# Scores inside chunks in two visits of four and three levels, and the pairs' seven products reordered with one bank for each two-part sum

## The chip, the cores and the metric

The kernel runs on one core of a Trainium2 chip. The metric is device time in microseconds (us) of one execution; lower is better. The core has a matrix engine (TensorE, in the profile PE for matmuls and PEld for weight loads), three other compute engines (VectorE = DVE, ScalarE = ACT, GpSimd = POOL), a queue for transfers (SyncE = SP), an on-chip memory, and PSUM, eight banks of 128 x 512 fp32 into which TensorE writes its products and from which DVE and ACT read them.

## The reference

One block on 1040 tokens (16 meta tokens and 1024 others) of width 1024: a norm, one wide projection, a pooling mixer beside chunked gated linear attention, gates, an output projection, and a squared-ReLU MLP. The change touches the projection and the attention's work inside a chunk of 64 tokens (4 heads, 64 key and 128 value channels each):

```python
z = jnp.einsum('bld,dn->bln', u, w_in)
a, q, k, v, r, lr, ga, gb = jnp.split(z, IN_SPLITS, axis=-1)
...
b = jnp.cumsum(ac, axis=2)
decay = jnp.exp(-jnp.abs(b[:, :, :, None, :] - b[:, :, None, :, :]))
scores = jnp.einsum('bhtk,bhsk,bhtsk->bhts', qc, kc, decay)
o = jnp.einsum('bhts,bhsv->bhtv', scores, vc) + jnp.einsum('bhtk,bhkv->bhtv', qc * jnp.exp(b), S)
```

Each score has a decay of its own for every pair of tokens and key channel, so `scores` isn't a plain product.

## The kernel before

Stages follow each other: norm, transposes and value projection (`start`), the first projections (`first_products`), **the projections in pairs with the scores between them (`pairs_of_projections`, some 141 to 376 us)**, the states across chunks, the output projection and the MLP. The change is in the third one.

*Products.* An fp32 matrix is split into a high and a low part (`split`, L977: ACT copies to the high part, L982, DVE subtracts it for the low part, L983), and `mm3` (L296) makes a product from three matmuls for each of 4 slices of the contraction, 12 of 128 x 512 (L300 to L302). The order on TensorE is the program's own (`manual_schedule` for PE); the order on DVE, ACT, POOL and SP in this stage is set by the framework's planner, and each of these engines works its own queue in order.

*Pairs.* Eleven pairs of 128-column weight blocks (`PAIRS`, L959: q, four of the gate gb, four of ga, two of r) are each multiplied by seven products P1 to P7 in place of eight (a Strassen-Winograd scheme). P1 and P2 add up in one bank (`xb`), P5 and P3 in another (`zb`), while P6, P7 and P4 take banks of tag `y` in turn. From these DVE makes `u2` (P1 + P6), `u3` (u2 + P7), and the four results: P1 + P2 (read from `xb` at P2's end), `zb` + u3 (L1102, after P5 and P7), P4 + u3 (L1112) and `zb` + u2 (L1116, after P3). They go through `put_q`, `put_gate` or `put_r` (ACT's tanh at L942, for r also a DVE product) to memory. `pairs_order` (L1006) sets the order P6 P1 P7 P5 P4 P2 P3, in which P1, P5 and P2 belong to the pair after that of the others. Two banks lie under the tag `sc`, two under `z`, two under `y`, two under `gs`.

*Weights of the products.* `sums_weights` (L1014) makes sums of weight blocks on GpSimd in halves (L1018) and splits them, three products ahead (`ahead`), into four slots. P5's sum is made into `fs`, P6's follows in place from it, P7's difference goes to `s3`, P3's again into `fs`. The next pair but one is loaded after P3.

*Scores.* `inside(p, half)` (L1208) is a unit: two heads, 512 tokens; there are four. It loads k, q (into two thirds of the tile `gi`) and the decay g, and builds operands for six levels of a binary tree over the 64 tokens: `grow` (L1229) makes level l + 1's operand pair from level l's with two DVE products (L1235, L1237), an ACT copy (L1236) and a small product of the decays (L1239), first from L1224 and L1227, at the end `last` (L1241). A level's score product (`scores`, L1191) is 16 matmuls on 64 x 64 quarters of the array, which the profile lists as 32; the first one has no decay (the token itself). They go to half of the two banks `gs`, half by half in turn. The first result is copied into `gi` by ACT (L1258), the others are laid in under a mask by DVE (`inlay`, L1255). Operands alternate between two tiles N, so a level's `grow` overwrites what the score product of the level before read. The filled `gi` goes to memory (L1279), and the next unit's loads go into the same tile (L1217 to L1219).

*How both are woven.* After each product with n > 8, `credit` grows by 12 x 512 / 2400 / 1.9 = 1.347, and while it is positive the chain `insides` goes on by a step, whose `yield` is taken off. A **visit** is a step in which TensorE makes score products. A unit has four of them: own and level 0, levels 1 and 2, levels 3 and 4, level 5. After each of the first two units `meta_state` makes that head pair's state from the meta tokens, with a transpose (L1177) and two small products (L1184), each in a step of its own.

Of the kernel before, what the change touches and what calls it, by code (L numbers as in the profile page):

```python
# [14 lines left out]
P = 128  # L15
D = 1024
SEQ = 1024
META = 16
# [10 lines left out]
VP = 272  # L29
NPAIR = DFF // P // 2  # L30
MP = 264
PACE, LEVEL, OPENING, STRETCH = 1.3, 1.6, 6.0, 1.9


class Stack:
# [87 lines left out]
def kernel(  # L123
# [30 lines left out]
    def bank(tag):  # L154
        if tag == "sc":
            sc_n[0] += 1
            return two("sc")[:, sc_n[0] % 2]
        return psp[tag].tile([P, 512], F32, name=f"b_{tag}", tag=tag)

    def two(tag):  # L160

        if tag in ("sc", "gs"):
            if tag not in wide:
                wide[tag] = psp[tag].tile([P, 2, 512], F32, name=f"b_{tag}", tag=tag)
            return wide[tag]
        return psp[tag].tile([P, 2, 512], F32, name=f"b_{tag}", tag=tag)
# [837 lines left out]
                    yield p, n  # L1004

    def pairs_order(n_pairs):  # L1006
        yield from (("P1", 0), ("P4", 0), ("P2", 0), ("P5", 0))
        for i in range(1, n_pairs + 1):
            for p in ("P6", "P1", "P7", "P5", "P4", "P2", "P3"):
                n = i if p in ("P1", "P5", "P2") else i - 1  # L1010
                if n < n_pairs and (p, n) != ("P4", 0):
                    yield p, n

    def sums_weights(order, n_pairs, load, eng):  # L1014

        def tt(out, a, b, op):
            for k in (slice(0, 2), slice(2, 4)) if eng is pool else (slice(0, 4),):
                eng.tensor_tensor(out[:, k], a[:, k], b[:, k], op)  # L1018

        for p, i in order(n_pairs):  # L1020
            a11, a12 = (w1raw[i, 0][:, k : k + 4] for k in (0, 4))
            if p in ("P1", "P2"):
                s = a11 if p == "P1" else a12
            else:
                a21, a22 = (w1raw[i, 1][:, k : k + 4] for k in (0, 4))
                s = None if p == "P4" else quad(S["fs"][:, i % 2] if p != "P7" else S["s3"])
                if p == "P5":
                    tt(s, a21, a22, ALU.add)
                elif p == "P6":
                    tt(s, s, a11, ALU.subtract)  # L1030
                elif p == "P7":
                    tt(s, a11, a21, ALU.subtract)
                elif p == "P3":
                    tt(s, a12, s, ALU.subtract)
                elif p == "P4":
                    s = a22
            yield p, i, split(s)
            if p == "P3" and i + 2 < n_pairs:
                load(i + 2, 0)
                load(i + 2, 1)  # L1040
# [8 lines left out]
    def first_pair():  # L1049
        raw.lend(*S["rawp"])  # L1050
        raw.slots = raw.slots[2:] + raw.slots[:2]
        raw.n = 0
        load_pair(0, 0)
        load_pair(0, 1)
        w1_slots()
        S["pw"] = sums_weights(pairs_order, len(PAIRS), load_pair, pool)

    def pair_weights():
        yield from S["first"]
# [2 lines left out]
    def pairs_of_projections():  # L1062
# [3 lines left out]
        S["fs"] = right.push("fs", [P, 2, HALF], F32)  # L1066
        S["s3"] = right.push("s3", [P, HALF], F32)
        S["u2p"] = right.push("u2p", [P, 2, HALF], F32)
        S["u3p"] = right.push("u3p", [P, 2, HALF], F32)
        load(1, 0)  # L1070
        load(1, 1)
        S["N"] = [right.push(f"n{i}", [P, HALF, 2], F32) for i in range(2)]
        S["F"] = right.push("f", [P, HALF, 2], F32)
        S["ends"] = right.push("ends", [P, HALF], F32)
        S["g"] = right.push("g", [P, HALF], F32)
        S["gi"] = right.push("gi", [P, 3, HALF], F32)
        banks(keep=1, y=2, gs=1, z=2)
        x, xb, zb = S["xs"], {}, {}
        total = 7 * len(PAIRS)
        chain, credit = insides(), 0.0  # L1080
        for n, (p, i, (ah, al)) in enumerate(ahead(pair_weights(), 3)):
            bh, bl = x[p]
            if p in ("P1", "P2"):
                b = xb[i] = bank("sc") if p == "P1" else xb[i]
            elif p in ("P5", "P3"):
                b = zb[i] = bank("z") if p == "P5" else zb[i]
            else:
                b = bank("y")
            more = p in ("P2", "P3")
            mm3(b, 4, lambda k: (ah[:, k], al[:, k]), lambda k: (bh[:, k], bl[:, k]), first=not more, more=more)  # L1090
            u2, u3 = S["u2p"][:, i % 2], S["u3p"][:, i % 2]
            put, d = PAIRS[i][1:]
            if p == "P1":
                act.activation(u2, b, ACT.Copy)
            elif p == "P2":
                put(d, 0, xb.pop(i), None)
            elif p == "P6":
                dve.tensor_tensor(u2, b, u2, ALU.add)
            elif p == "P7":
                dve.tensor_tensor(u3, b, u2, ALU.add)  # L1100
                c = nxt("c")
                dve.tensor_tensor(c, zb[i], u3, ALU.add)  # L1102
                put(d + 1, 1, c, c)
                if i == 0:
                    c = nxt("c")
                    dve.tensor_tensor(c, S["ends"], u3, ALU.add)
                    put(d + 1, 0, c, c)
            elif p == "P4" and i == 0:
                act.activation(S["ends"], b, ACT.Copy)
            elif p == "P4":  # L1110
                c = nxt("c")
                dve.tensor_tensor(c, b, u3, ALU.add)  # L1112
                put(d + 1, 0, c, c)
            elif p == "P3":
                c = nxt("c")
                dve.tensor_tensor(c, zb.pop(i), u2, ALU.add)  # L1116
                put(d, 1, c, c)
            if n > 8:
                credit += 12 * 512 / 2400 / STRETCH
# [44 lines left out]
        dve.tensor_tensor(sv[:, :, 0], sv[:, :, 0], end(1), ALU.add)  # L1164
        dve.tensor_tensor(pv[:, :, 1], pv[:, :, 1], end(0), ALU.add)

    def meta_state(p):
        pre, suf, y, km = (metab[:, i] for i in (META_LOG[p], 1, 2, 4))
        nc.sync.dma_start(km, k_dram[p, :, :META])
        dve.memset(suf, 0.0)  # L1170
        for m in (1, 2, 4, 8):
            twice(pre, suf, m)
        act.activation(y, suf, ACT.Exp, scale=1.0 / TAU)
        dve.tensor_tensor(y, y, km, ALU.mult)
        yield 5.0
        b = two("gs")[:, 0]
        pe.transpose(b[:META, :P], y, ident)  # L1177
        kt = gB[32 : 32 + META, 2 * 256 : 2 * 256 + P]
        dve.tensor_copy(kt, b[:META, :P])
        yield 2.0  # L1180
        b = two("gs")[:, 0]
        for e in range(2):
            r = slice(e * CH, (e + 1) * CH)
            pe.matmul(  # L1184
                b[r, :P], kt[:, r], vm[:, (2 * p + e) * P : (2 * p + e + 1) * P], start=True, stop=True,
                tile_position=(32, e * CH),
            )
        dve.tensor_copy(S["S"][:, 0, p], b[:, :P])
        yield 1.0

    def scores(kk, qq):  # L1191


        turn_n[0] += 1
        c = (turn_n[0] % 2) * 4 * CH
        b = two("gs")[:, :, c : c + 4 * CH].rearrange("p e (j t) -> p e j t", j=4)
        for j in range(4):
            for e, u in QUARTERS:
                r, to, s = part(e), part(u), part(2 * j + u)
                pe.matmul(b[to, e, j], kk[r, s], qq[r, s], start=True, stop=True, tile_position=(e * CH, u * CH))  # L1200
        return b
# [6 lines left out]
    def inside(p, half):  # L1208
# [8 lines left out]
        nc.sync.dma_start(gi[:, 1], k_dram[p, :, at : at + HALF])  # L1217
        nc.sync.dma_start(gi[:, 2], q_dram[p, half])
        nc.sync.dma_start(g, decay_dram[p, half])  # L1219
        yield 4.5  # L1220
        pairs = lambda a: a.rearrange("p (b u) n -> p b u n", u=2)
        plain, gp = kq.rearrange("p n (b u) -> p b u n", u=2), g.rearrange("p (b u) -> p b u", u=2)
        for u, to, other in ((1, N[0], F), (0, F, N[0])):
# [25 lines left out]
                act.activation(o[:, :, 1 - u], f[:, :, 1 - u], ACT.Copy)  # L1249
            dve.tensor_tensor(e2, ev[:, :, 0], ev[:, :, 1], ALU.mult)  # L1250

        yield 2.0

        def inlay(lvl, b):
            dve.copy_predicated(scc, mask[:, lvl : lvl + 1, None, :].broadcast_to([P, 2, 4, CH]), b)  # L1255

        b = [scores(kq[:, 0], kq[:, 1]), scores(N[0][:, :, 0], N[0][:, :, 1])]
        act.activation(scc, b[0], ACT.Copy)  # L1258
        inlay(0, b[1])
        e, at = g, 0  # L1260
        for lvl in range(6):
            m, n = 1 << lvl, N[lvl % 2]
            to = at + HALF // (2 * m)
            e2 = ends[:, at:to] if lvl < 5 else dec_of(p, half)
            if lvl < 5:
                grow(m, n, N[1 - lvl % 2], e, e2)
            e2_of, e, at = (e, e2), e2, to
            if lvl < 5:
                yield LEVEL
            if lvl in (1, 3):  # L1270
                b = [scores(N[i][:, :, 0], N[i][:, :, 1]) for i in (1, 0)]
                for i in range(2):
                    inlay(lvl + i, b[i])
            elif lvl == 5:
                b = scores(n[:, :, 0], n[:, :, 1])
                last(n, *e2_of)
                inlay(5, b)
        yield LEVEL
        nc.sync.dma_start(gi_dram[p, half], gi)  # L1279

    def insides():
        for half in range(2):
            for p in range(2):
                yield from inside(p, half)
                if half == 0:
                    yield from meta_state(p)

    step(one, pairs_of_projections)

# [660 lines left out]
```

## Time and profile before

| | |
|---|---|
| median of 3 runs (lowest, highest) | 1198.33 us (1198.26, 1198.54) |
| profiled execution, its own time | 1198.67 us |
| its span | 1195.8 us |
| granted TensorE clock, mean | 0.998 |
| HBM read and written | 128.66 and 62.93 MB, 160 GB/s over the span |

The profile shows one execution. For an engine it gives the time that it was busy, the share of the span and the instructions; for a group of instructions the line, engine, operation, out<-in by the program's names, shapes, count, busy time, mean ns of one, and the idle time just before them with what ended it. In a timeline each row has start and duration; matmuls are pipelined, so a duration reaches past the next one's start and the pace is read from starts. Of TensorE's chain that ended last 69% of the span is TensorE's own work.

### The profile page before, as it was taken

Reading aid. Unit: us, or ns where it says so; the run is one execution under the profiler, and the core shown is the slowest. Engines: PE = TensorE matmul, PEld = TensorE weight load, DVE = VectorE, ACT = ScalarE, POOL = GpSimd, SP = SyncE. Lnnn points to the kernel's source line nnn. Section 1 sums busy time; section 2 is a strip of 40 time slices with the busy share of each in tenths; the row PEclk is TensorE's granted clock in tenths of the full one; section 3 lists DMA queues with packets and bytes.
Section 4 is the critical chain, followed back from the end, with each engine's and each line's share of the span. In section 5 each row is a group of like instructions: output and inputs, shape, how many; then the busy total and the mean of one; then the engine's idle time right before and its main releaser. Section 6 shows DMA issues by size and latency. Waiting matters only on the chain.

```text
span 1195.8 us, 18439 instructions
## 1 busy us (share of the span) xinstructions
PE 1182.6 (99%) x6823; PEld 982.5 (82%) x6823; DVE 853.6 (71%) x1400; ACT 579.0 (48%) x1006; POOL 102.1 (9%) x121
## 2 busy tenths in 40 slices
PE   9999999999999999999999999999999999999997
PEld 7999887777778887888788888888888888888886
DVE  7679657565676779527986766777675887887686
ACT  7566544444456224216754555545454444445454
POOL 0224232333220000000000000000000000000000
PEclk9999999999999999999999999999999999999999
DMA  8232533434357879712254544445389963333532
GB/s 247 69 89 81 180 112 113 143 125 142 124 168 265 293 229 306 257 34 89 89 185 143 165 146 163 153 139 167 132 285 336 328 213 97 97 97 97 168 97 88
DMA packets 151001, 192.79 MB, mean 161 GB/s; under 512 B 12088, under 2 KB 85616, under 8 KB 150912
## 3 DMA queue, kind: packets, MB, share of 16 engines
q1 hardware_dynamic: 150752, 191.56, 50.1%
q8 instruction: 53, 0.87, 0.3%
q14 instruction: 36, 0.29, 0.1%
q10 hardware_dynamic: 160, 0.07, 0.0%
HBM read 128.66 MB, written 62.93 MB: 160 GB/s over the span
## 4 chain that ended last, share of the span: by engine, by line
PE 69%; DVE 3%; issue 1%; ACT 1%; DMA 0%; DVEq 0%
PE b_oa L300 5%; PE b_oa L302 5%; PE b_oa L301 5%; PE b_y L300 4%; PE b_mm L300 4%; PE b_y L301 4%; PE b_y L302 4%; PE b_mm L302 4%; PE b_mm L301 4%; PE b_ob L300 4%; PE b_ob L302 4%; PE b_ob L301 4%; PE b_z L301 3%; PE b_z L300 3%; PE b_z L302 3%; PE b_sc L300 2%
## 5 line engine op out<-in xcount | busy, mean ns | idle before, releaser
L300 PE MATMUL b_z<-th,w1h 128*128 128x512 f32 x240 | 94.3, 393 | 0.0
L301 PE MATMUL b_z<-tl,w1h 128*128 128x512 f32 x240 | 93.6, 390 | 0.4 <-DVE tl L1617 0.4
L302 PE MATMUL b_z<-th,w1l 128*128 128x512 f32 x240 | 93.5, 390 | 0.0
L982 ACT ACTIVATE w1h<-raw 128x512 fp32r<-128x512 f32 x103 | 64.0, 622 | 54.9 <-PE b_y L301 23.1
L300 PE MATMUL b_sc<-th,w1h 128*128 128x512 f32 (+1 forms) x232 | 89.8, 387 | 0.7 <-ACT u2p L1733 0.7
L301 PE MATMUL b_sc<-tl,w1h 128*128 128x512 f32 (+1 forms) x232 | 89.2, 385 | 0.0
L302 PE MATMUL b_sc<-th,w1l 128*128 128x512 f32 (+1 forms) x232 | 89.0, 383 | 0.0
L983 DVE TENSOR_TENSOR w1l<-raw,w1h 128x512 fp32r<-128x512 f32 x103 | 70.6, 686 | 18.4 <-ACT w1h L982 18.4
L982 ACT ACTIVATE w1h<-fs 128x512 fp32r<-128x512 f32 x81 | 51.1, 631 | 65.8 <-PE b_y L301 34.2
L983 DVE TENSOR_TENSOR w1l<-fs,w1h 128x512 fp32r<-128x512 f32 x81 | 56.2, 694 | 21.8 <-ACT w1h L982 21.6
L982 ACT ACTIVATE w1h<-bt 128x512 fp32r<-128x512 f32 x46 | 29.1, 632 | 70.8 <-issue 43.9
L1809 DVE TENSOR_TENSOR bt<-w,w 128x512 f32<-128x512 f32 x80 | 54.6, 683 | 0.6 <-DMA w<-in_w_ff_dram 0.6
L301 PEld LDWEIGHTS b_z<-tl,w1h 128*128 128x128 f32 x240 | 45.1, 188 | 9.9 <-DVE tl L1617 0.8
L300 PEld LDWEIGHTS b_z<-th,w1h 128*128 128x128 f32 x240 | 45.0, 188 | 9.8 <-issue 0.2
L302 PEld LDWEIGHTS b_z<-th,w1l 128*128 128x128 f32 x240 | 45.1, 188 | 9.7
L300 PEld LDWEIGHTS b_sc<-th,w1h 128*128 128x128 f32 x232 | 43.6, 188 | 10.4 <-ACT u2p L1733 1.2
L302 PEld LDWEIGHTS b_sc<-th,w1l 128*128 128x128 f32 x232 | 43.6, 188 | 8.8
L301 PEld LDWEIGHTS b_sc<-tl,w1h 128*128 128x128 f32 x232 | 43.6, 188 | 8.6
L300 PE MATMUL b_mm<-wo,th 128*128 128x512 f32 x128 | 50.4, 393 | 0.0
L983 DVE TENSOR_TENSOR w1l<-bt,w1h 128x512 fp32r<-128x512 f32 x46 | 31.7, 690 | 25.6 <-ACT w1h L982 25.6
L302 PE MATMUL b_mm<-wo,tl 128*128 128x512 f32 x128 | 49.9, 390 | 0.0
L301 PE MATMUL b_mm<-wo,th 128*128 128x512 f32 x128 | 49.8, 389 | 0.0
(535 smaller groups left out, 3405.7 us busy)
## 6 DMA issues: line engine op xcount, KB each, us to landing
hf_dram<-h SPq DMA_DIRECT2D x112, 256.0 KB, 2.1
raw<-hf_dram SPq DMA_DIRECT2D x112, 256.0 KB, 2.7
w<-in_w_ff_dram SPq DMA_DIRECT2D x64, 256.0 KB, 4.6
raw<-in_w_in_dram SPq DMA_DIRECT2D x18, 512.0 KB, 4.8
raw<-in_w_ff_dram SPq DMA_DIRECT2D x16, 512.0 KB, 4.2
rawx<-in_w_ff_dram SPq DMA_DIRECT2D x16, 512.0 KB, 4.1
rawp<-in_w_in_dram SPq DMA_DIRECT2D x14, 512.0 KB, 4.8
xs<-in_x_dram SPq DMA_DIRECT2D x8, 512.0 KB, 5.4
```

What stands on the lines that cost most here:

```text
L300: pe.matmul(ps, ah, bh, start=first and i == 0, stop=False, skip_group_check=more)
L301: pe.matmul(ps, ah, bl, start=False, stop=False, skip_group_check=more)
L302: pe.matmul(ps, al, bh, start=False, stop=last and i == n - 1, skip_group_check=more)
L982: act.activation(hi, a, ACT.Copy)
L983: dve.tensor_tensor(lo, a, f32(hi), ALU.subtract)
L1809: dve.tensor_tensor(bt, w, S["w2"][q[3:]][:, i], ALU.add if q[2] == "+" else ALU.subtract)
```

## The change

1. `inside` has two visits in place of four. The first makes four score products (own, levels 0 to 2), the second three (levels 3 to 5). There are three operand tiles N in place of two, so that three levels' operands stand at a time. `scores` is told its place: four halves of two pairs of banks, `gs` and `g2`. The inlays of levels 0 to 2 follow `grow` steps 2 to 4, those of levels 3 to 5 the second visit. The small decay products alternate between `ends` and the tile g, which is thus in use for longer. The steps' costs (`yield`) are other ones, 16.0 a unit in place of 16.1.
2. `meta_states` handles both head pairs at once behind the second unit: one visit of two transposes, one of four small products.
3. The banks for `g2` come from `z`. `xb` and `zb` are now the two banks of `sc`, one each for all pairs. `u3p` holds one buffer; P4 of the first pair goes to g in place of `ends`.
4. `pairs_order` becomes P6 P1 P5 P7 P4 P2 P3, with P5 now of the same pair as P6 and P7. `pair_sums` makes P6's two sums in one go (`s3`, then `fs` from it), gives `s3` to P5, and then makes P7's difference in `s3`. The MLP keeps `sums_weights`.

```diff
-PACE, LEVEL, OPENING, STRETCH = 1.3, 1.6, 6.0, 1.9
+PACE, OPENING, STRETCH = 1.3, 6.0, 1.9
...
     def pairs_order(n_pairs):
-        yield from (("P1", 0), ("P4", 0), ("P2", 0), ("P5", 0))
+        yield from (("P1", 0), ("P4", 0), ("P2", 0))
         for i in range(1, n_pairs + 1):
-            for p in ("P6", "P1", "P7", "P5", "P4", "P2", "P3"):
-                n = i if p in ("P1", "P5", "P2") else i - 1
+            for p in ("P6", "P1", "P5", "P7", "P4", "P2", "P3"):
+                n = i if p in ("P1", "P2") else i - 1
...
+    def pair_sums(n_pairs, load):
+
+        for p, i in pairs_order(n_pairs):
+            a11, a12 = (w1raw[i, 0][:, k : k + 4] for k in (0, 4))
+            if p in ("P1", "P2"):
+                s = a11 if p == "P1" else a12
+            else:
+                a21, a22 = (w1raw[i, 1][:, k : k + 4] for k in (0, 4))
+                if p != "P4":
+                    f, s3 = quad(S["fs"][:, i % 2]), quad(S["s3"])
+                if p == "P6":
+                    s = f
+                    in_halves(s3, a21, a22, ALU.add)
+                    in_halves(f, s3, a11, ALU.subtract)
+                elif p == "P5":
+                    s = s3
+                elif p == "P7":
+                    s = s3
+                    in_halves(s3, a11, a21, ALU.subtract)
+                elif p == "P3":
+                    s = f
+                    in_halves(f, a12, f, ALU.subtract)
+                else:
+                    s = a22
+            yield p, i, split(s)
+            if p == "P3" and i + 2 < n_pairs:
+                load(i + 2, 0)
+                load(i + 2, 1)
...
-        S["u3p"] = right.push("u3p", [P, 2, HALF], F32)
+        S["u3p"] = right.push("u3p", [P, HALF], F32)
-        S["N"] = [right.push(f"n{i}", [P, HALF, 2], F32) for i in range(2)]
+        S["N"] = [right.push(f"n{i}", [P, HALF, 2], F32) for i in range(3)]
-        S["ends"] = right.push("ends", [P, HALF], F32)
+        S["ends"] = right.push("ends", [P, 384], F32)
-        banks(keep=1, y=2, gs=1, z=2)
-        x, xb, zb = S["xs"], {}, {}
+        banks(keep=1, y=2, gs=1, g2=1)
+        x, xb, zb = S["xs"], two("sc")[:, 0], two("sc")[:, 1]
...
-            if p in ("P1", "P2"):
-                b = xb[i] = bank("sc") if p == "P1" else xb[i]
-            elif p in ("P5", "P3"):
-                b = zb[i] = bank("z") if p == "P5" else zb[i]
-            else:
-                b = bank("y")
+            b = xb if p in ("P1", "P2") else zb if p in ("P5", "P3") else bank("y")
...
+    def meta_states():
+        y = [metab[:, i] for i in (2, 5)]
+        for p in range(2):
...
         yield 5.0
         b = two("gs")[:, 0]
-        pe.transpose(b[:META, :P], y, ident)
+        for p in range(2):
+            pe.transpose(b[:META, p * P : (p + 1) * P], y[p], ident)
...
-        yield 2.0
+        yield 3.0
...
-    def scores(kk, qq):
-        turn_n[0] += 1
-        c = (turn_n[0] % 2) * 4 * CH
-        b = two("gs")[:, :, c : c + 4 * CH].rearrange("p e (j t) -> p e j t", j=4)
+    def scores(place, kk, qq):
+        c = (place % 2) * 4 * CH
+        b = two("g2" if place > 1 else "gs")[:, :, c : c + 4 * CH].rearrange("p e (j t) -> p e j t", j=4)
...
-        yield 4.5
+        yield 4.0
...
-        yield 2.0
+        yield 1.0
...
-        b = [scores(kq[:, 0], kq[:, 1]), scores(N[0][:, :, 0], N[0][:, :, 1])]
-        act.activation(scc, b[0], ACT.Copy)
-        inlay(0, b[1])
-        e, at = g, 0
-        for lvl in range(6):
-            m, n = 1 << lvl, N[lvl % 2]
...
-            if lvl < 5:
-                grow(m, n, N[1 - lvl % 2], e, e2)
-            e2_of, e, at = (e, e2), e2, to
-            if lvl < 5:
-                yield LEVEL
-            if lvl in (1, 3):
-                b = [scores(N[i][:, :, 0], N[i][:, :, 1]) for i in (1, 0)]
-                for i in range(2):
-                    inlay(lvl + i, b[i])
-            elif lvl == 5:
-                b = scores(n[:, :, 0], n[:, :, 1])
-                last(n, *e2_of)
-                inlay(5, b)
-        yield LEVEL
+        e, b = g, {}
+        for lvl in range(5):
+            e2 = (ends[:, :256], g[:, :128], ends[:, 256:320], g[:, 128:160], ends[:, 320:336])[lvl]
+            grow(1 << lvl, N[lvl % 3], N[(lvl + 1) % 3], e, e2)
+            e = e2
+            if lvl > 1:
+                inlay(lvl - 2, b.pop(lvl - 2))
+            yield (1.4, 1.6, 2.0, 2.0, 2.4)[lvl]
+            if lvl == 1:
+                own = scores(0, kq[:, 0], kq[:, 1])
+                for n in range(3):
+                    b[n] = scores(1 + n, N[n][:, :, 0], N[n][:, :, 1])
+                act.activation(scc, own, ACT.Copy)
+        for n in range(3):
+            b[3 + n] = scores(n, N[n][:, :, 0], N[n][:, :, 1])
+        last(N[2], e, dec_of(p, half))
+        for n in range(3, 6):
+            inlay(n, b.pop(n))
+        yield 1.6
         nc.sync.dma_start(gi_dram[p, half], gi)
...
             for p in range(2):
                 yield from inside(p, half)
-                if half == 0:
-                    yield from meta_state(p)
+            if half == 0:
+                yield from meta_states()
```

More of the change, by code (lines that the diff above doesn't have):

```diff
@@ L160, in two @@
     def two(tag):
-        if tag in ("sc", "gs"):
+        if tag in ("sc", "gs", "g2"):
             if tag not in wide:
@@ L1006, in pairs_order @@
     def pairs_order(n_pairs):
-        yield from (("P1", 0), ("P4", 0), ("P2", 0), ("P5", 0))
+        yield from (("P1", 0), ("P4", 0), ("P2", 0))
         for i in range(1, n_pairs + 1):
-            for p in ("P6", "P1", "P7", "P5", "P4", "P2", "P3"):
-                n = i if p in ("P1", "P5", "P2") else i - 1
+            for p in ("P6", "P1", "P5", "P7", "P4", "P2", "P3"):
+                n = i if p in ("P1", "P2") else i - 1
                 if n < n_pairs and (p, n) != ("P4", 0):
                     yield p, n
+    def pair_sums(n_pairs, load):
[25 more added lines that the diff above has]
+                load(i + 2, 1)
     def sums_weights(order, n_pairs, load, eng):
-        def tt(out, a, b, op):
-            for k in (slice(0, 2), slice(2, 4)) if eng is pool else (slice(0, 4),):
-                eng.tensor_tensor(out[:, k], a[:, k], b[:, k], op)
+        tt = eng.tensor_tensor
         for p, i in order(n_pairs):
@@ L1055, in first_pair @@
         w1_slots()
-        S["pw"] = sums_weights(pairs_order, len(PAIRS), load_pair, pool)
+        S["pw"] = pair_sums(len(PAIRS), load_pair)
     def pair_weights():
@@ L1082, in pairs_of_projections @@
             bh, bl = x[p]
-            if p in ("P1", "P2"):
-                b = xb[i] = bank("sc") if p == "P1" else xb[i]
-            elif p in ("P5", "P3"):
-                b = zb[i] = bank("z") if p == "P5" else zb[i]
-            else:
-                b = bank("y")
+            b = xb if p in ("P1", "P2") else zb if p in ("P5", "P3") else bank("y")
             more = p in ("P2", "P3")
             mm3(b, 4, lambda k: (ah[:, k], al[:, k]), lambda k: (bh[:, k], bl[:, k]), first=not more, more=more)
-            u2, u3 = S["u2p"][:, i % 2], S["u3p"][:, i % 2]
+            u2, u3 = S["u2p"][:, i % 2], S["u3p"]
             put, d = PAIRS[i][1:]
@@ L1095, in pairs_of_projections @@
             elif p == "P2":
-                put(d, 0, xb.pop(i), None)
+                put(d, 0, xb, None)
             elif p == "P6":
@@ L1101, in pairs_of_projections @@
                 c = nxt("c")
-                dve.tensor_tensor(c, zb[i], u3, ALU.add)
+                dve.tensor_tensor(c, zb, u3, ALU.add)
                 put(d + 1, 1, c, c)
@@ L1105, in pairs_of_projections @@
                     c = nxt("c")
-                    dve.tensor_tensor(c, S["ends"], u3, ALU.add)
+                    dve.tensor_tensor(c, S["g"], u3, ALU.add)
                     put(d + 1, 0, c, c)
             elif p == "P4" and i == 0:
-                act.activation(S["ends"], b, ACT.Copy)
+                act.activation(S["g"], b, ACT.Copy)
             elif p == "P4":
@@ L1115, in pairs_of_projections @@
                 c = nxt("c")
-                dve.tensor_tensor(c, zb.pop(i), u2, ALU.add)
+                dve.tensor_tensor(c, zb, u2, ALU.add)
                 put(d, 1, c, c)
@@ L1165, in twice @@
         dve.tensor_tensor(pv[:, :, 1], pv[:, :, 1], end(0), ALU.add)
[L1167 to L1174, printed above, removed]
+    def meta_states():
+        y = [metab[:, i] for i in (2, 5)]
+        for p in range(2):
+            pre, suf, km = (metab[:, i] for i in (META_LOG[p], 1, 4))
+            nc.sync.dma_start(km, k_dram[p, :, :META])
+            dve.memset(suf, 0.0)
+            for m in (1, 2, 4, 8):
+                twice(pre, suf, m)
+            act.activation(y[p], suf, ACT.Exp, scale=1.0 / TAU)
+            dve.tensor_tensor(y[p], y[p], km, ALU.mult)
@@ L1175, in meta_state @@
         yield 5.0
         b = two("gs")[:, 0]
-        pe.transpose(b[:META, :P], y, ident)
-        kt = gB[32 : 32 + META, 2 * 256 : 2 * 256 + P]
-        dve.tensor_copy(kt, b[:META, :P])
-        yield 2.0
-        b = two("gs")[:, 0]
[L1182 to L1187, printed above, removed]
@@ L1188, in meta_state @@
-        dve.tensor_copy(S["S"][:, 0, p], b[:, :P])
+        for p in range(2):
+            pe.transpose(b[:META, p * P : (p + 1) * P], y[p], ident)
+        kt = gB[32 : 32 + META, 2 * 256 : 2 * 256 + 2 * P]
+        dve.tensor_copy(kt, b[:META, : 2 * P])
+        yield 3.0
+        b = two("gs")[:, 0]
+        for p in range(2):
+            for e in range(2):
+                n = 2 * p + e
+                pe.matmul(
+                    b[e * CH : (e + 1) * CH, p * P : (p + 1) * P], kt[:, n * CH : (n + 1) * CH],
+                    vm[:, n * P : (n + 1) * P], start=True, stop=True, tile_position=(32, e * CH),
+                )
@@ L1189, in meta_state @@
+        dve.tensor_copy(S["S"][:, 0], b[:, : 2 * P].rearrange("p (a c) -> p a c", a=2))
         yield 1.0
-    def scores(kk, qq):
-        turn_n[0] += 1
-        c = (turn_n[0] % 2) * 4 * CH
-        b = two("gs")[:, :, c : c + 4 * CH].rearrange("p e (j t) -> p e j t", j=4)
+    def scores(place, kk, qq):
+        c = (place % 2) * 4 * CH
+        b = two("g2" if place > 1 else "gs")[:, :, c : c + 4 * CH].rearrange("p e (j t) -> p e j t", j=4)
         for j in range(4):
@@ L1250, in last @@
             dve.tensor_tensor(e2, ev[:, :, 0], ev[:, :, 1], ALU.mult)
-        yield 2.0
+        yield 1.0
         def inlay(lvl, b):
             dve.copy_predicated(scc, mask[:, lvl : lvl + 1, None, :].broadcast_to([P, 2, 4, CH]), b)
-        b = [scores(kq[:, 0], kq[:, 1]), scores(N[0][:, :, 0], N[0][:, :, 1])]
-        act.activation(scc, b[0], ACT.Copy)
-        inlay(0, b[1])
-        e, at = g, 0
-        for lvl in range(6):
-            m, n = 1 << lvl, N[lvl % 2]
-            to = at + HALF // (2 * m)
-            e2 = ends[:, at:to] if lvl < 5 else dec_of(p, half)
-            if lvl < 5:
-                grow(m, n, N[1 - lvl % 2], e, e2)
-            e2_of, e, at = (e, e2), e2, to
-            if lvl < 5:
-                yield LEVEL
-            if lvl in (1, 3):
-                b = [scores(N[i][:, :, 0], N[i][:, :, 1]) for i in (1, 0)]
-                for i in range(2):
-                    inlay(lvl + i, b[i])
-            elif lvl == 5:
-                b = scores(n[:, :, 0], n[:, :, 1])
-                last(n, *e2_of)
-                inlay(5, b)
-        yield LEVEL
+        e, b = g, {}
[17 more added lines that the diff above has]
+        yield 1.6
         nc.sync.dma_start(gi_dram[p, half], gi)
```

## The prediction

> **What bounds the kernel now.** First the page's opening lines, then the stretch that the change touches (141 to 354 us, the projections in pairs with the score chain between them), then who TensorE waits for there. The middle row gives length, busy time of PE, PEld, DVE, ACT and POOL (instructions), granted clock, DMA share and GB/s; a wait its total, count and longest.
>
> ```profile
> span 1195.8 us, 18439 instructions
> PE 1182.6 (99%) x6823; PEld 982.5 (82%) x6823; DVE 853.6 (71%) x1400; ACT 579.0 (48%) x1006; POOL 102.1 (9%) x121
> ```
> ```profile
> 141.00:354.00 213.00, 211.47 (x1732) 168.94 (x1731) 134.90 (x225) 95.72 (x161) 65.46 (x80) 1.00 0.43 132
> ```
> ```profile
> PE b_gs L1200 <- DVE gi L1255: 0.9, 2, 0.7
> PE b_gs L1200 <- ACT gi L1249: 0.5, 1, 0.5
> ```
>
> TensorE is busy 99% of the span; in the stretch it is busy 211.47 of 213 us at granted clock 1.00, and the only listed waits are 1.4 us in front of score products (L1200). So a microsecond of DVE, ACT or DMA is worth nothing here while TensorE keeps running. Worth something are only instructions of TensorE, the gaps between them that count as busy, and waits that appear or go. The next view is TensorE's timeline around one visit of two score products (start, duration):
>
> ```profile
> 329.78 0.39 PE L302 MATMUL b_y<-t1h,w1l 128*128 128x512 f32 x1
> 330.10 0.69 PE L1200 MATMUL b_gs<-gi 64*64 64x64 f32 x32
> 330.62 0.66 PE L1200 MATMUL b_gs<-n 64*64 64x64 f32 x32
> 331.21 0.50 PE L300 MATMUL b_z<-th,w1h 128*128 128x512 f32 x1
> 331.55 0.39 PE L301 MATMUL b_z<-tl,w1h 128*128 128x512 f32 x1
> ...
> 255.44 0.39 PE L302 MATMUL b_z<-th,w1l 128*128 128x512 f32 x1
> 256.55 0.71 PE L1200 MATMUL b_gs<-n 64*64 64x64 f32 x32 [0.72 <-DVE gi L1255]
> 257.19 0.50 PE L300 MATMUL b_y<-t0h,w1h 128*128 128x512 f32 x1
> ```
>
> Read starts, not durations. A visit of two products holds TensorE from 330.10 to 331.21 (1.11), of one from 256.55 to 257.19 (0.64): one more product costs 0.47. From the last wide matmul before to the second one after, 329.78 to 331.55, pass 1.77 us. Taking off 0.94 for two products and 0.46 for two ordinary steps (0.23 each: the products quoted further down take twelve steps in 2.75 and 2.80) leaves **0.37 us that belong to the visit itself**. An ordinary visit begins 0.32 after the wide matmul before it (329.78 to 330.10); this single-product visit begins 1.11 after (255.44 to 256.55), so 0.79 of it is a wait, listed as 0.72. The three listed waits of such last visits (1.4 us) with 0.07 more each make 1.6 us.
>
> **The change part by part.**
>
> *Visits.* Four units have four visits each (2, 2, 2 and 1 products), afterwards two (4 and 3). Score products stay 28. Eight visits go: 8 x 0.37 = **-3.0 us**. It could be less if part of the 0.37 came with every product; the step 330.10 to 330.62 shows at most 0.05 between products, so the lower end is 8 x 0.32 = 2.6.
>
> *Meta states.* Their transposes and products merge from four visits to two.
>
> ```profile
> 220.45 0.39 PE L302 MATMUL b_y<-t1h,w1l 128*128 128x512 f32 x1
> 220.77 0.43 PE L1184 MATMUL b_gs<-gB 16*64 16x128 f32 x4
> 221.13 0.50 PE L300 MATMUL b_z<-th,w1h 128*128 128x512 f32 x1
> 221.47 0.39 PE L301 MATMUL b_z<-tl,w1h 128*128 128x512 f32 x1
> ```
>
> 220.45 to 221.47 less two steps is 0.56, of which I give 0.37 to the visit as above and the rest to the four matmuls, which stay. The transposes are whole-array matmuls like those around them; I take nothing for their merging. Together **-0.4** (between -0.2 and -0.6).
>
> *The last visit's wait.* Now the sixth level follows one product (credit 1.6 against 1.347 a product) behind a visit whose operand buffer it overwrites. Afterwards the second visit comes 2.0 + 2.0 + 2.4 = 6.4 credits, four to five products, behind the first, with a third operand buffer. What is late next is the chain between the visits (busy us, mean ns | idle before and its releaser):
>
> ```profile
> L1255 DVE COPY_PREDICATED gi<-mask,b_gs 128x512 f32<-128x512 uint8 x24 | 17.6, 735 | 0.6 <-ACT gi L1258 0.6
> L1237 DVE TENSOR_TENSOR f<-n,ends 128x512 f32<-128x512 f32 x16 | 13.6, 850 | 0.1
> L1236 ACT ACTIVATE n<-f 128x512 f32<-128x512 f32 x20 | 12.7, 637 | 6.1 <-DVE f L1237 5.2 <-PE b_gs L1200 0.6 <-DVE f L1224 0.3
> L1235 DVE TENSOR_TENSOR n<-n,ends 128x512 f32<-128x512 f32 x16 | 10.9, 680 | 0.0
> L983 DVE TENSOR_TENSOR w1l<-raw,w1h 128x512 fp32r<-128x512 f32 x15 | 10.5, 699 | 6.1 <-ACT w1h L982 6.1
> L1018 POOL TENSOR_TENSOR s<-raw,raw 128x256 f32<-128x256 f32 x10 | 7.2, 737 | 20.0 <-DVE w1l L983 20.0
> ```
>
> It needs on DVE 3 x 0.68 (L1235), 2 x 0.85 (L1237), 2 x 0.74 (two inlays, whose bank places the next visit rewrites) and about 0.5 of small products: 5.7 us. The projections' own DVE work is seven splits and five sums of 0.69 per seven products, 1.18 a product, 4.7 for four. That is 10.4 against four products of 2.75 and most of a 2.2 us visit, 12.6. The cover holds with 2 us to spare; without it TensorE waits what is missing, four times. I count **-1.6**, at worst 0.
>
> *Order of the seven products.* Work is equal; only the pace can move, which hangs on the neighbour:
>
> ```profile
> 174.01 0.40 PE L300 MATMUL b_y<-t1h,w1h 128*128 128x512 f32 x1
> 176.81 0.40 PE L300 MATMUL b_z<-th,w1h 128*128 128x512 f32 x1
> ...
> 368.33 0.39 PE L300 MATMUL b_y<-t1h,w1h 128*128 128x512 f32 x1
> 371.08 0.40 PE L300 MATMUL b_y<-t2h,w1h 128*128 128x512 f32 x1
> ```
>
> P7 behind P1 took 2.80 us, behind another product 2.75. It now stands behind P5 in ten pairs: between -0.5 and +0.3, **-0.2** taken.
>
> *Sums on GpSimd.* Still eight half operations of 0.74 a pair, none new: P5's sum is now made with P6's, and P7's difference now overwrites the buffer that P5's split reads. So GpSimd starts P7's difference after that split (about 1.4 us from its slot's release), takes 1.5, and ACT's next split waits some 0.2 to 1 us. It is made three products (8 us) ahead; ACT is idle over half the time. Cost 0.
>
> *One bank for each two-part sum.* P1 must wait until the previous P2's sum is read, P5 until P3's is: two products, 5.5 us, lie between.
>
> ```profile
> L1116 DVE TENSOR_TENSOR c<-b_z,u2p 128x512 f32<-128x512 f32 x9 | 6.2, 689 | 9.6 <-PE b_z L302 9.6
> L1102 DVE TENSOR_TENSOR c<-b_z,u3p 128x512 f32<-128x512 f32 x9 | 6.1, 682 | 0.0
> ```
>
> DVE mostly sits idle until P3 ends (9.6 us over nine) and then reads for 0.69. Inside a pair P7's read (two sums, some 1.9 us with a split between) must precede P3, also 5.5 us later. Cost 0, with a rival below. [...]
>
> *The handover between units.* Two of the three are now direct (the first loses the meta work between its units, the last had none): store of `gi`, loads into it, the first products, and then the first visit, which now wants N[2] too. The last handover of before shows the price (start, duration; the last two rows: KB, us to landing):
>
> ```profile
> 312.60 0.71 PE L1200 MATMUL b_gs<-n 64*64 64x64 f32 x32 [0.55 <-ACT gi L1249]
> ```
> ```profile
> 316.05 0.52 SPq L1279 DMA_DIRECT2D gi_dram<-gi  x1
> ```
> ```profile
> 326.15 0.83 DVE L1224 TENSOR_TENSOR n<-gi,g 128x512 f32<-128x512 f32 x1 [3.03 <-DMA gi<-q_dram]
> ...
> 332.66 0.68 DVE L1235 TENSOR_TENSOR n<-n,ends 128x512 f32<-128x512 f32 x1
> ```
> ```profile
> g<-decay_dram SPq DMA_DIRECT2D x4, 256.0 KB, 5.0
> gi<-q_dram SPq DMA_DIRECT2D x4, 256.0 KB, 3.8
> ```
>
> Visit to store 3.45, store to first product 10.1, and 7.2 until the operand of the third level is there (333.34). Its shortest chain is two L1224, two L1235, one L1237 and a small one, 4.3. Two more inlays and longer scores put the store at 3.5 to 5.2. So N[2] is ready 17.9 to 22.5 us after the last visit began. TensorE gets there after 1.7 and seven products (1.6 + 4.0 + 1.0 + 1.4 + 1.6 = 9.6 credits, over 1.347 = 7.1) of 2.75: 21.0. The wait is 0 to 1.5; the load of `g`, which is now in use up to the fourth level and so may queue behind k and q on SP (0.4 later, and 5.0 instead of 3.8 to land), can add 1.6. I take 0.45 at each of two handovers: **+0.9**, between 0 and 6. Behind the waiting score product stands all of TensorE; DVE and ACT in turn hold a sum and a split behind the loads, which have 5.5 and 8 us.
>
> **Sum.** -3.0 - 0.4 - 1.6 - 0.2 + 0.9 = -4.3 us. The profiled execution took 1198.67 (span 1195.8 and 2.9 around it), 0.3 above the median 1198.33. From the median: **1194.0 us**. What a measurement of this kernel tells from no change is 0.2%, 2.4 us.
>
> **Rivals.**
>
> 1. *Handovers become the bound.* For it: DVE already idled 3.03 us for that load, and the first handover loses 8 credits of meta work. Against: seven products lie between. With the store at 4.4, `g` late by 1.6 and the chain at 7.2, N[2] comes at 23.3, 2.3 late; twice that in place of 0.9 makes the sum -0.6: 1197.7.
>
> 2. *The visit's cost does not go with the visit*, but with the score products. For it: a visit's matmuls are pipelined and their ends modelled. Against: the 0.47 for a further product. Then 3.0 is lost: 1197.0.
>
> 3. *A bank comes back late: slower.* DVE works in its queue's order. If the read of the sum stands behind the split of the product whose slot is freed only when P1 ends, it starts 5.5 + 0.63 (ACT) + 0.69 us after P3 and ends 0.69 later: P5 is 2.0 us late. Three of the 20 returns so placed eat the gain, four give -4.3 + 8.0 = +3.7: 1202.0. For it: one bank each, a DVE that is busy 134.9 of 213 us, and its 3 us hold for loads. Against: the read now stands right behind P3, 4.7 us early. [...]
>
> **How the numbers follow.** Forecast 0.62 (own range 1192.1 to 1195.9), first rival 0.15, second 0.08, third 0.12, more gain than forecast 0.03. Faster by over 0.2% (below 1195.9): 0.62 + 0.03 = 0.65. Within: 0.15 + 0.08 = 0.23. Slower: 0.12. The range leaves out the third rival, the extra gain and the upper tail of the first: 1192.1 to 1198.1.
>
> **What would show it.** Right: visits of 128 and 96 score matmuls, nine gaps of some 0.37 fewer, no wait at L1200's second visits, and the stretch some 4.3 us shorter. Wrong: waits `PE b_gs` or `b_g2` on DVE n L1235 or ACT n L1236 before the second and fourth units' first visits (first rival); unchanged busy time of the stretch (second); waits `PE b_sc` L300 on DVE c or ACT t (third). A shift outside 141 to 354 us would mean that the order planned for DVE and ACT later on moved, which I count at nothing.

## The result: slower by 2.9%, and the profile after

| | before | after |
|---|---|---|
| median (lowest, highest) | 1198.26 us (1197.19, 1198.54), 5 runs | 1233.31 us (1230.20, 1234.94), 5 runs |
| profiled execution, its own time | 1198.67 us | 1230.2 us |

The ratio after to before is 1.0289, 95% interval 1.0278 to 1.03. The forecast was 1194.0 us, its range 1192.1 to 1198.1: the time lies outside, on the other side.

The opening lines of the page after:

```profile
span 1228.4 us, 18429 instructions
PE 1188.7 (97%) x6823; PEld 984.4 (80%) x6823; DVE 858.9 (70%) x1398; ACT 579.2 (47%) x1006; POOL 106.0 (9%) x121
```

The span grew by 32.6 us and TensorE's busy time by 6.1. So most of what came is idle time of TensorE, which the changed matmuls don't explain: there are as many as before, 6823. The table of windows for 141 to 395 us (length, busy us of PE, PEld, DVE, ACT, POOL, granted clock, DMA share, GB/s) puts it in the stage of the change:

```profile
141.00:395.00 254.00, 226.64 (x1772) 178.39 (x1771) 150.49 (x238) 105.52 (x174) 71.97 (x84) 0.98 0.39 122
```

TensorE is idle for 27.4 of these 254 us, where before it was idle for 1.5 of 213, and the granted clock is 0.98 in place of 1.00. What it waits for stands in the table of TensorE's waits (total us, times, longest):

```profile
PE b_sc L300 <- ACT u2p L1115: 9.9, 8, 3.2
PE b_sc L300 <- ACT t L942: 9.1, 7, 3.0
PE b_sc L300 <- DVE c L953: 6.0, 2, 3.4
PE b_sc L300 <- DVE c L1123: 2.2, 1, 2.2
```

Four rows, 18 waits, 27.2 us. All stand in front of the first matmul (L300) of a product that goes to `b_sc`, the tile that now holds both `xb` and `zb`. None stands in front of a score product. L1115 is the copy of P1's sum, L942 and L953 are the tanh and the product that read P1 + P2, and L1123 is the read of `zb` behind P7; the product that waits for that one is P2 of the second pair, which writes `xb`. One of the first kind, in TensorE's and ACT's timeline (start, duration):

```profile
199.10 0.40 PE L301 MATMUL b_sc<-tl,w1h 128*128 128x512 f32 x1
199.34 0.39 PE L302 MATMUL b_sc<-th,w1l 128*128 128x512 f32 x1
199.59 0.63 ACT L982 ACTIVATE w1h<-raw 128x512 fp32r<-128x512 f32 x1 [0.63 <-PE b_sc L301]
200.13 0.58 ACT L1115 ACTIVATE u2p<-b_sc 128x512 f32<-128x512 f32 x1
200.76 0.50 PE L300 MATMUL b_sc<-th,w1h 128*128 128x512 f32 x1 [1.04 <-ACT u2p L1115]
201.10 0.40 PE L301 MATMUL b_sc<-tl,w1h 128*128 128x512 f32 x1
```

P1's last matmul starts at 199.34. ACT's queue holds a split first (199.59), then the copy of `xb`, which ends at 200.71. At 200.76 P5 begins, **which writes the other bank, `zb`**, and needs nothing of that copy. A step, from one matmul's start to the next one's, of 0.23 has become 1.42, and the next step takes 0.34. And one of the second kind, where P3 stands behind P2 (TensorE and ACT):

```profile
237.95 0.39 PE L302 MATMUL b_sc<-th,w1l 128*128 128x512 f32 x1
...
239.82 0.43 ACT L1272 ACTIVATE gi<-f 128x256 f32<-128x256 f32 x1 [0.57 <-DVE f L1260]
240.15 0.61 ACT L982 ACTIVATE w1h<-s 128x512 fp32r<-128x512 f32 x1
240.67 0.58 ACT L942 ACTIVATE t<-b_sc 128x512 f32<-128x512 f32 x1
...
241.30 0.79 PE L300 MATMUL b_sc<-th,w1h 128*128 128x512 f32 x1 [2.97 <-ACT t L942]
```

The tanh that reads `xb` stands third in ACT's queue, behind a copy of the score chain that itself waits for DVE. It ends at 241.25, and only then does P3 go on in `zb`, 3.35 us after P2's last matmul began.

The gap in the profiled spans can be put together from these rows. The listed waits are 27.2. Each step is 0.15 longer than its listed wait and an ordinary step (1.42 - 1.04 - 0.23), and the step behind it 0.11 longer (0.34 - 0.23): 18 x 0.26 = 4.7. Matmuls at half clock behind three of the long waits cost 4.5 more (last section). That is 36.4. The two-tile kernel below has all of the change but these waits. Its span is 1191.9, so 36.5 shorter, with one wait of its own that costs 1.0 (0.7 and 0.26), so 1.1 us stay unassigned.

### The profile page after: what moved, and what is told of

Same layout as the page of the kernel before. It is cut to its first block, busy times and chain, and to the rows that moved or that the text cites. A ratio compares the mean times of both kernels' runs of the same rounds, so it can differ in the third digit from the quotient of the medians.

```text
span 1228.4 us, 18429 instructions
## 1 busy us (share of the span) xinstructions
PE 1188.7 (97%) x6823; PEld 984.4 (80%) x6823; DVE 858.9 (70%) x1398; ACT 579.2 (47%) x1006; POOL 106.0 (9%) x121
## 4 chain that ended last, share of the span: by engine, by line
PE 75%; DVE 5%; DMA 3%; ACT 2%; issue 2%; SPq 0%; DVEq 0%; ACTq 0%
PE b_y L300 5%; PE b_y L302 5%; PE b_y L301 5%; PE b_sc L300 5%; PE b_sc L301 5%; PE b_oa L302 5%; PE b_oa L301 5%; PE b_oa L300 5%; PE b_sc L302 4%; PE b_mm L300 4%; PE b_mm L302 4%; PE b_mm L301 4%; PE b_ob L301 4%; PE b_ob L302 4%; PE b_ob L300 4%; PE b_z L301 2%
## 5 line engine op out<-in xcount | busy, mean ns | idle before, releaser
L300 PE MATMUL b_sc<-th,w1h 128*128 128x512 f32 (+1 forms) x320 | 128.0, 400 | 27.9 <-ACT u2p L1115 9.9
L301 PE MATMUL b_sc<-tl,w1h 128*128 128x512 f32 (+1 forms) x320 | 125.3, 392 | 0.0
L302 PE MATMUL b_sc<-th,w1l 128*128 128x512 f32 (+1 forms) x320 | 125.0, 391 | 0.0
L300 PEld LDWEIGHTS b_sc<-th,w1h 128*128 128x128 f32 x320 | 61.1, 191 | 48.6 <-ACT u2p L1115 13.1
L302 PEld LDWEIGHTS b_sc<-th,w1l 128*128 128x128 f32 x320 | 61.2, 191 | 13.0
L301 PEld LDWEIGHTS b_sc<-tl,w1h 128*128 128x128 f32 x320 | 61.3, 191 | 11.9
L301 PE MATMUL b_z<-tl,w1h 128*128 128x512 f32 x152 | 59.3, 390 | 0.4 <-DVE tl L1637 0.4
L300 PE MATMUL b_z<-th,w1h 128*128 128x512 f32 x152 | 59.3, 390 | 0.1
L302 PE MATMUL b_z<-th,w1l 128*128 128x512 f32 x152 | 59.2, 389 | 0.0
L300 PE MATMUL b_mm<-wo,th 128*128 128x512 f32 x128 | 50.4, 393 | 0.0
L300 PE MATMUL b_y<-wo,w1h 128*128 128x512 f32 x128 | 49.8, 389 | 0.0
L301 PE MATMUL b_y<-wo,w1h 128*128 128x512 f32 x128 | 49.8, 389 | 0.0
L302 PE MATMUL b_y<-wo,w1l 128*128 128x512 f32 x128 | 49.8, 389 | 0.0
```

The lines of the kernel that those rows point to most:

```text
L300: pe.matmul(ps, ah, bh, start=first and i == 0, stop=False, skip_group_check=more)
L301: pe.matmul(ps, ah, bl, start=False, stop=False, skip_group_check=more)
L302: pe.matmul(ps, al, bh, start=False, stop=last and i == n - 1, skip_group_check=more)
```

## The experiments

The theory after this reading, A in the expectations: the framework orders accesses by tile, so the two halves of one tile `sc` count as one object, and a product that writes `zb` waits for the last read of `xb`. The new order puts P5 right behind P1 and P3 right behind P2, where such a read is always still to come. The rivals: the loss comes with the order or with two banks fewer as such (a sum's own bank comes back late, as the prediction's third rival had it), or with the merged visits.

**Two tiles.** The changed kernel, with each sum's bank a tile of its own. Order, visits and the number of banks stay.

```diff
-        banks(keep=1, y=2, gs=1, g2=1)
-        x, xb, zb = S["xs"], two("sc")[:, 0], two("sc")[:, 1]
+        banks(xb=1, zb=1, y=2, gs=1, g2=1)
+        x, xb, zb = S["xs"], bank("xb"), bank("zb")
...
-        banks(keep=1, mm=4, m2=1)
+        banks(sc=1, mm=4, m2=1)
```

> The changed kernel with the two sums in two tiles of one bank each in place of two halves of one tile; same banks, same order of products, same visits. Theory A (the halves of one tile are ordered as one, so P5 waits until P1's copy in the other bank is done and P3 until P2's sum in the other bank is read): the waits of TensorE in front of b_sc (some 27 us) go, and with them the slow matmuls behind the longest of them; the time falls from 1233 to what the prediction had for the rest, 1192 to 1196. Theory B (one bank a sum: the same bank comes back too late, two products after its last use): the waits stay under the new names, 1228 to 1236. Theory C (several edits share the loss): in between, 1200 to 1225.

Measured: 1193.74 us (1193.24 to 1194.34, 5 runs), ratio to before 0.9964, interval 0.995 to 0.9977. The same stretch, and the one new wait in the table of TensorE's waits:

```profile
141.00:395.00 254.00, 253.25 (x2051) 205.28 (x2049) 171.84 (x276) 115.95 (x189) 71.22 (x84) 1.00 0.52 164
```
```profile
PE b_zb L300 <- DVE c L1123: 0.7, 1, 0.7
```

Idle time falls from 27.4 to 0.75 us, and the clock is 1.00 again. The place that answers to 199.34 above, in the two-tile kernel's timeline:

```profile
194.15 0.39 PE L302 MATMUL b_xb<-th,w1l 128*128 128x512 f32 x1
194.38 0.40 PE L300 MATMUL b_zb<-th,w1h 128*128 128x512 f32 x1
194.41 0.63 ACT L982 ACTIVATE w1h<-raw 128x512 fp32r<-128x512 f32 x1 [0.56 <-PE b_xb L301]
194.95 0.58 ACT L1115 ACTIVATE u2p<-b_xb 128x512 f32<-128x512 f32 x1
```

P5 starts 0.23 behind P1, and TensorE writes `zb` while ACT reads `xb` (194.95 to 195.53). The same split and the same copy stand on ACT, as late as before; nobody waits for them. So the chip did not ask for the wait; the program had it. The two-tile kernel is faster than both others, 0.4% below before and 3.2% below after (1193.74 / 1233.31).

**The order without the visits, in one tile.** The kernel before, with `pairs_order` and `pair_sums` of the change and the two sums in one tile; four visits a unit and everything else as before.

```diff
...
-        x, xb, zb = S["xs"], {}, {}
+        x, xb, zb = S["xs"], two("sc")[:, 0], two("sc")[:, 1]
...
+            b = xb if p in ("P1", "P2") else zb if p in ("P5", "P3") else bank("y")
...
-        S["pw"] = sums_weights(pairs_order, len(PAIRS), load_pair, pool)
+        S["pw"] = pair_sums(len(PAIRS), load_pair)
```

> The kernel before with the new order of the seven products and the two sums in two halves of one tile, but the old four visits a unit. A: the whole loss is here without the visits; 30 to 40 us over before, 1228 to 1240, with waits in front of b_sc on ACT u2p, ACT t and DVE c. If the visits or the handovers between units made the loss: 1197 to 1200.

Measured: 1232.38 us (1229.69 to 1233.07, 4 runs), ratio 1.0282, interval 1.0268 to 1.0296. TensorE's waits of this kernel (L1118 and L1126 are the lines L1115 and L1123 of the kernel after):

```profile
PE b_sc L300 <- ACT u2p L1118: 9.0, 8, 2.0
PE b_sc L300 <- ACT t L942: 7.5, 7, 1.4
PE b_sc L300 <- DVE c L953: 6.9, 2, 5.4
PE b_sc L300 <- DVE c L1126: 3.2, 1, 3.2
```

The same four rows with the same counts: the whole loss is there without a visit changed.

**The order with the banks before.** As the last kernel, but with `sc` and `z` as before, two banks for each sum.

```diff
-            for p in ("P6", "P1", "P7", "P5", "P4", "P2", "P3"):
-                n = i if p in ("P1", "P5", "P2") else i - 1
+            for p in ("P6", "P1", "P5", "P7", "P4", "P2", "P3"):
+                n = i if p in ("P1", "P2") else i - 1
...
-        S["pw"] = sums_weights(pairs_order, len(PAIRS), load_pair, pool)
+        S["pw"] = pair_sums(len(PAIRS), load_pair)
```

> The kernel before with the new order of the seven products and of their weight sums alone, the banks as before (two in turn for either sum). A: within 1 us of before, 1197.5 to 1199, by the term of -0.2 us for the pace. If the order or GpSimd's sums cost something of their own: above 1200.

Measured: 1199.89 us (1199.36 to 1201.45, 11 runs), ratio 1.0016, interval 1.0007 to 1.0025. The order alone is not what costs 34 us. But the time is above the expected one, by a little. Its waits (L1229 is the line of the score products here, L1284 that of the inlays):

```profile
PE b_gs L1229 <- DVE gi L1284: 1.6, 1, 1.6
...
PE b_z L300 <- DVE c L1131: 1.2, 1, 1.2
...
PE b_gs L1229 <- ACT gi L1278: 0.6, 1, 0.6
```

The last visits' waits are 2.2 us in place of 1.4, and P3 of the first pair waits 1.2 for the read of its own bank behind P7 (L1131). Together 2.0, against 1.7 that the order cost (1199.89 - 1198.22).

**P5 ahead of P1.** The changed kernel, one tile, with P5 moved away from P1's copy; P3 stays behind P2.

```diff
-            for p in ("P6", "P1", "P5", "P7", "P4", "P2", "P3"):
+            for p in ("P6", "P5", "P1", "P7", "P4", "P2", "P3"):
```

> The changed kernel with P5 ahead of P1 (P6 P5 P1 P7 P4 P2 P3), still one tile. The two banks are still written in direct succession there, but no read of the tile comes between P5 and P1; P3 still follows P2's read. A: the waits on ACT u2p (9.9 us, and those of its kind) go, those of P3 on ACT t and DVE c stay: 1208 to 1222. If the succession of two groups in neighbouring banks costs by itself: no change, 1228 to 1236. If the bank's own return (B): P5 now comes one product after P3's sum is read, so more waits there, 1235 or more.

Measured: 1219.58 us (1218.65 to 1219.94, 4 runs), ratio 1.0178, interval 1.0164 to 1.0192. Its waits:

```profile
PE b_sc L300 <- ACT t L942: 9.4, 7, 3.2
PE b_sc L300 <- DVE c L953: 6.0, 2, 3.4
PE b_sc L300 <- DVE c L1123: 2.3, 2, 2.1
```

The row of `u2p` is gone and the others stand, within 0.3 us. So each of the two neighbourhoods costs by itself; the first is worth 13.7 us (1233.31 - 1219.58), of which 9.9 are listed and 8 x 0.26 = 2.1 follow from the steps around them. The profiled executions lie closer together, 10.7 (spans 1228.4 and 1217.7), since the profiled one of the kernel after is its fastest.

**Four visits again.** The two-tile kernel, with each visit cut in two and one projection product between the halves; the sum of credits stays.

```diff
-            yield (1.4, 1.6, 2.0, 2.0, 2.4)[lvl]
+            yield (1.4, 1.6, 0.65, 2.0, 1.05)[lvl]
...
-                act.activation(scc, own, ACT.Copy)
+                    if n == 0:
+                        act.activation(scc, own, ACT.Copy)
+                        yield 1.35
         for n in range(3):
             b[3 + n] = scores(n, N[n][:, :, 0], N[n][:, :, 1])
+            if n == 1:
+                yield 1.35
```

> The two-tile kernel (e1_two_tiles, 1193.74) with each unit's two score visits of 4 and 3 products split again into four of 2, 2, 2 and 1, one projection product between the halves, the same products and the same sum of credits: eight visits more. The prediction's price of 0.37 us a visit gives 8 x 0.37 = 3.0 us more: 1196.7, between 1195.8 and 1197.6, with the ratio to before 0.998 to 0.9995, and TensorE's listed waits in front of score products unchanged at 0. The rival (the price goes with the score products, not the visits) gives 1193.7, 1193.0 to 1194.5. If waits in front of score products appear, their sum is to be taken off first.

Beside it the two-tile kernel ran once more on the same chip.

> The same kernel as e1_two_tiles once more, on the chip of e5_four_visits, as its reference: 1193.7, within 1 us of it, ratio to before 0.995 to 0.998.

Measured: 1196.02 us (1195.42 to 1196.74, 11 runs), ratio 0.9986, interval 0.9977 to 0.9994, against 1193.64 (1192.65 to 1194.14, 5 runs), ratio 0.9961, interval 0.9948 to 0.9975, for the two-tile kernel on that chip. Eight visits cost 2.38 us, **0.30 each**, near the lower end that the prediction gave (0.32) and below its 0.37. The runs of the two kernels lie between 1.3 and 4.1 us apart (0.16 to 0.51 a visit), so the exact price stays open; a price of nothing (1193.7 expected by the rival) does not fit, the runs don't overlap. Two split visits on TensorE's timeline of the kernel with four visits:

```profile
183.27 0.70 PE L1223 MATMUL b_gs<-gi 64*64 64x64 f32 x32
183.79 0.66 PE L1223 MATMUL b_gs<-n 64*64 64x64 f32 x32
184.38 0.50 PE L300 MATMUL b_zb<-th,w1h 128*128 128x512 f32 x1
...
187.01 0.39 PE L302 MATMUL b_zb<-th,w1l 128*128 128x512 f32 x1
187.32 1.19 PE L1223 MATMUL b_g<-n 64*64 64x64 f32 x64
188.44 0.50 PE L300 MATMUL b_y<-t0h,w1h 128*128 128x512 f32 x1
188.78 0.39 PE L301 MATMUL b_y<-t0l,w1h 128*128 128x512 f32 x1
```

By these starts a visit of two products takes 187.01 to 188.78 = 1.77 us up to the second wide matmul, as before the change, from which the prediction worked out 0.37; the kernel's time shows 0.30. Neither visit waits.

## Why the prediction was wrong, step by step

**The step that failed is "One bank for each two-part sum", cost 0.** It gave each sum a bank and asked when that bank comes back: "P1 must wait until the previous P2's sum is read, P5 until P3's is: two products, 5.5 us, lie between." With two tiles that held: the one wait listed there, 0.7 us, is inside a pair. But `xb` and `zb` are two halves of one tile, and in this program a write to either half comes behind the last read of the other. So P5 waited for P1's copy and P3 for P2's tanh, reads that can't start before the product right ahead of them ends. The constraint could be read in the diff, `two("sc")[:, 0]` and `[:, 1]`, where before the change `zb` had a tag of its own. In the kernel before, the `xb` of one pair and of the next lay in one tile too, but two other products lay between the read of the one and the first matmul of the other, so its trace had no such wait in front of a sum. It did show the like in front of a score product, in a row that the prediction put down to another cause: at 256.55 TensorE begins a unit's last one, after a wait for an inlay. VectorE's timeline of the kernel before has the two inlays ahead of it:

```profile
254.72 0.74 DVE L1255 COPY_PREDICATED gi<-mask,b_gs 128x512 f32<-128x512 uint8 x1
...
255.68 0.72 DVE L1255 COPY_PREDICATED gi<-mask,b_gs 128x512 f32<-128x512 uint8 x1
```

The halves of `gs` are taken in turn, so the last product writes the half that the first of these inlays read, until 255.46. Its operands were ready by 253.64 (L1235 and L1236). It begins 0.15 after the second inlay, which reads the other half, ended at 256.40. So a write to one half already waited for the read of the other. Both halves of `gs` lie in the same two banks, so this row alone can't tell an ordering by tile from one by bank.

**The third rival** had the right sign and named the right waits (`PE b_sc` L300 on ACT t and DVE c), at a chance of 0.12, but another mechanism and price: a bank's own return, 2.0 us late at four places, 1202.0. The waits came at 18 places and for the neighbouring bank. At none of the 20 returns does the two-tile kernel list a wait. A read that stands late in DVE's queue did hold up TensorE at one place, inside a pair: P3 of the first pair adds to the bank that is read behind P7. That comes with the order, not with one bank for each sum, as the kernel with the banks before has it too (1.2 us). The two-tile kernel's timeline, VectorE and TensorE:

```profile
161.55 0.69 DVE L983 TENSOR_TENSOR w1l<-fs,w1h 128x512 fp32r<-128x512 f32 x1 [5.15 <-ACT w1h L982]
162.16 0.68 DVE L1121 TENSOR_TENSOR u3p<-b_y,u2p 128x512 f32<-128x512 f32 x1
162.76 0.85 DVE L983 TENSOR_TENSOR w1l<-rawp,w1h 128x512 fp32r<-128x512 f32 x1
...
163.54 0.68 DVE L1123 TENSOR_TENSOR c<-b_zb,u3p 128x512 f32<-128x512 f32 x1
...
164.27 0.50 PE L300 MATMUL b_zb<-th,w1h 128*128 128x512 f32 x1 [0.75 <-DVE c L1123]
```

Here P4 is made early, so only P2 lies between P7 and P3, and two splits stand ahead of the sums in DVE's queue. The prediction's "also 5.5 us later" held for ten pairs and not for the first.

**The other terms** can be read from the two-tile kernel, whose 1193.74 and 1193.64 lie at the forecast 1194.0:

| term | predicted | measured | from |
|---|---|---|---|
| eight visits | -3.0 | -2.4 | split visits against two tiles |
| meta states | -0.4 | not tried alone | |
| last visits' waits | -1.6 | -1.6 | no wait left at L1223; the size is the prediction's |
| order of the products | -0.2 | +1.7 with the old visits | order with the banks before |
| of it with two tiles | | +1.0 | wait of P3, first pair, 0.7 listed and 0.26 around it |
| handovers | +0.9 | 0 | no wait at L1223 |
| one bank for each sum, as halves of one tile | 0 | +39.6 | 1233.31 - 1193.74 |

With 0.4 for the meta states the terms of the two-tile kernel make -2.4 - 0.4 - 1.6 + 1.0 = -3.4, and measured are -4.5 (1193.74 against 1198.22 on its chip) and -4.1 (1193.64 against 1197.7). The remaining 0.7 to 1.1 isn't assigned. That two tiles come out at the forecast is thus partly luck: visits worth 0.6 less and the first pair's wait of 1.0 stand against handovers that cost 0.9 less. The last visits' waits went, but the prediction had their cause wrong: it named the chain and the operand buffer, and the rows above have the product begin behind the inlay of the other half. The first rival (handovers) and the second (the visit's price does not go with the visit) fell.

## What to carry to other kernels

When two buffers are made halves of one tile, list for each write which reads of the other half come before it: the ordering may go by the tile, as it did here (18 waits, 27.2 us), whatever the banks allow. A bank for each sum was enough here, where two other products, 5.5 us, lay between its uses and each sum had a tile of its own: none of the 20 returns waited. And a wait that a change might add is to be priced at every place where the pattern repeats: here most cost 1.3 us (1.19 in the long step and 0.11 in the next), and there are 18.

## What the runs showed of the hardware beside it

After three of the long waits TensorE ran at half clock. TensorE's timeline of the kernel after, from P3's start at 241.30, and the windows behind the four waits whose step was 3.0 us or more (237.95, 345.18, 361.63 and 386.56):

```profile
241.89 0.63 PE L301 MATMUL b_sc<-tl,w1h 128*128 128x512 f32 x1
242.31 0.63 PE L302 MATMUL b_sc<-th,w1l 128*128 128x512 f32 x1
242.74 0.63 PE L300 MATMUL b_sc<-th,w1h 128*128 128x512 f32 x1
...
244.83 0.40 PE L302 MATMUL b_sc<-th,w1l 128*128 128x512 f32 x1
245.06 0.40 PE L300 MATMUL b_sc<-th,w1h 128*128 128x512 f32 x1
```
```profile
241.30:244.40 3.10, 3.10 (x7) 2.47 (x8) 0.96 (x2) 0.27 (x1) 1.44 (x2) 0.51 0.48 159
...
349.20:352.30 3.10, 3.10 (x15) 2.52 (x14) 0.00 (x0) 0.56 (x1) 0.00 (x0) 1.00 0.20 61
364.60:367.70 3.10, 3.07 (x7) 2.48 (x8) 0.00 (x0) 0.00 (x0) 0.13 (x1) 0.51 0.57 163
390.30:393.40 3.10, 3.04 (x9) 2.38 (x10) 1.16 (x2) 0.00 (x0) 0.00 (x0) 0.70 0.33 126
```

Steps of 0.43 in place of 0.23 last for some 3 us, at a granted clock of 0.51. Behind the wait at 345.18, one of the longest (3.63 us from start to start), the clock stays at 1.00; behind the one of 3.00 at 361.63 it halves; behind the one of 3.80 at 386.56 it halves only after five matmuls, so the window shows 0.70, and the slow steps go on behind the window, to 395.0. By the starts the three stretches have 8, 7 and 8 slow steps. What these took above the usual 0.23, and above the 0.34 already counted behind a wait, is 1.58, 1.38 and 1.51, together 4.5 us. Not the length of the wait alone decides: listed waits of 2.6 and 3.0 us were followed by half clock at once, one of 3.4 after five matmuls, and one of 3.2 was not. What else decides, these rows don't show.
